# Two of five gate-and-up chunks as seven block products of sums, and one pool for the weight tiles

## The chip, the core and the metric

The kernel runs on one core of a Trainium2 chip. The metric is the time of one execution on the device in microseconds (us). The core has a matrix engine (TensorE, PE in the profile), three engines for elementwise work (VectorE, DVE; ScalarE, ACT; GpSimd, POOL) and queues that start transfers (SyncE, SP). They run beside each other, each in its own fixed order of instructions, and wait for each other by semaphores.

## The reference

256 tokens of 1024 features go through two blocks in float32. Block 1 is a feed-forward (f1), a mixer of neighbourhood attention and pools, a second feed-forward (f2) and a per-layer embedding (ple), each with a norm by the sum of squares before and after. Block 2 is twice: a feed-forward, a mixer (gated linear attention, gla, the first time; retention, ret, the second), a feed-forward, each followed by a layer norm of the weighted residual. Its four feed-forwards are called s0 to s3.

```python
def swiglu_2(x, w_in, w_out):
    gate, up = jnp.split(x @ w_in, 2, axis=-1)
    return (jax.nn.silu(gate) * up) @ w_out

    ...
    for i in range(DEPTH_2):
        h = layer_norm(DN_ALPHA * h + 0.5 * swiglu_2(h, ffn_w_in[i, 0], ffn_w_out[i, 0]), ln_g[i, 0], ln_b[i, 0])
        ...
        h = layer_norm(DN_ALPHA * h + m, ln_g[i, 1], ln_b[i, 1])
        h = layer_norm(DN_ALPHA * h + 0.5 * swiglu_2(h, ffn_w_in[i, 1], ffn_w_out[i, 1]), ln_g[i, 2], ln_b[i, 2])
```

The inner width of a feed-forward is 2816.

## The kernel before

**Operands.** Every float32 operand of a product is split in two tiles of type float32r that add up to it: `hi` is a copy (ScalarE), `lo` is the operand less `hi` (VectorE). A product of two operands is then three matmuls: hi by hi, hi by lo, lo by hi (`mm3`, L173). The tokens are two blocks of 128, t=0 and t=1.

**Weights.** They are streamed in units of 128x2048 elements, 1 MB. `fetch` (L143) starts the transfer of a unit to a tile `raw`, copies it to `whi` on ScalarE (L155) and subtracts on VectorE to `wlo` (L156). The pools hold 4 raw, 5 whi and 5 wlo tiles. `unit` (L159) hands out the next unit of a fixed plan and fetches one unit ahead.

**A feed-forward.** `ffn` (L336) computes gate and up in five chunks of 512 columns and a sixth of half the size. A chunk of 512 columns has four weight units (gate's two halves of the 1024 rows, up's two), and each serves both blocks of tokens: eight block products [128x512] by [512x512], each of 12 matmuls of 128x512. When a gate is complete, ScalarE makes `sg` (silu, L344 or L347); when the up product is complete, VectorE makes `pr` = up times `sg` (L345 or L348). Four ticks later (a tick is six matmuls) `pr` is transposed on TensorE and split in `hTh` (ScalarE, L192) and `hTl` (VectorE, L193). Then `lagged` (L296) multiplies by the down weight, 11 units of two rows of blocks: t=1 follows t=0 by three units (`LAG`), so that t=0's norm, which `after` starts, can run beside t=1's last products. The norms are `rms_post` (L247) and `rms_in` (L232) in block 1 and `ln_post` (L258) in block 2; `turn_in` (L243) defers the transposes of the normed tokens by `TURN` ticks, and these become `xTh` and `xTl`, the next layer's operand.

**Order.** The program is written as one stream in which `tick`, `defer` and `settle` place the deferred pieces. A scheduler then fixes for every engine one order of instructions, in which it takes account of when tiles of a pool come free. So a pool's size has a say in the order, and the order is what the engines keep to while they run. The file also has `proj` (L285), which multiplies one block of tokens by units, and `Chunks`, by which the mixers do the same as `ffn`.

Of the kernel before, what the change touches and what calls it, by code (L numbers as in the profile page):

```python
# [38 lines left out]
class Split:  # L39
    """A float32 operand as two float32r tiles that add up to it exactly."""  # L40
# [8 lines left out]
def ffn_units(g, u, d):  # L49
# [10 lines left out]

MIX_ORDER = [1, 0, 2, 3, 4, 5, 6, 7]
# [4 lines left out]
def all_units():  # L66
    """Every weight unit in the order of its use."""
# [4 lines left out]
    p += ffn_units("s0g", "s0u", "s0d")  # L72
    p += chunk_units("gin", GLA_ORDER) + [("gout", i) for i in range(4)]
    p += ffn_units("s1g", "s1u", "s1d") + ffn_units("s2g", "s2u", "s2d")
    p += chunk_units("rin", RET_ORDER) + [("rout", i) for i in range(8)]
    return p + ffn_units("s3g", "s3u", "s3d")


class Build:
# [152 lines left out]
    def rms_in(self, t, gpre):  # L232
        """The next layer's operand from h[t]: h * g, transposed and split, and its rstd."""
# [24 lines left out]
    def ln_post(self, t, acc, g, b, half, last=False):  # L258
        """h[t] = layer_norm(ALPHA * h + (0.5 if half else 1) * acc) * g + b; its transpose, split."""
# [13 lines left out]
        for n in range(2):  # L273
# [5 lines left out]
            else:  # L279
                self.turn_in(xT, t, n, y)  # L280
# [55 lines left out]
    def ffn(self, xT, r, wg, wu, wd, after, first=False):  # L336
# [14 lines left out]
        pss = {}  # L351
# [670 lines left out]
```

## Time and profile before

| | us |
|---|---|
| median of 3 runs | 1642.52 |
| lowest and highest run | 1640.35, 1642.58 |
| span of the profiled execution | 1639.3 |
| TensorE busy in it | 1622.8 |
| VectorE busy | 935.0 |
| ScalarE busy | 723.9 |
| GpSimd busy | 131.1 |

The span reaches from the first instruction to the last in one execution that the hardware profiler recorded; that execution's own time outside the span is not in the profile. A matmul's busy time in the profile overlaps its neighbour's, so the distance of two starts, not the duration, says how fast they follow each other. "Idle before, releaser" names the time an engine stood still ahead of an instruction and what ended it.

### The profile page before, as it was taken

The numbers are of one execution on the slowest core, as the hardware profiler recorded it, in microseconds if no ns is written. First come the engines' busy times: TensorE is split into PE (matmuls) and PEld (weight loads), VectorE is DVE, ScalarE is ACT, GpSimd is POOL, SyncE is SP. The second block draws the span as 40 slices with busy tenths as digits, with TensorE's granted clock in tenths as the row PEclk, the third lists the DMA queues.
The fourth block names the chain that finished last, engine by engine and source line by source line (L and its number), as shares of the span: only waits on it lengthen the run. The fifth ranks groups of instructions, "written<-read, shape, count | busy, mean of one in ns | idle before, by whom it ended". The sixth has DMA issues, their size and how long they took to land.

```text
span 1639.3 us, 18199 instructions
## 1 busy us (share of the span) xinstructions
PE 1622.8 (99%) x7512; PEld 1339.8 (82%) x7512; DVE 935.0 (57%) x809; ACT 723.9 (44%) x712; POOL 131.1 (8%) x149
## 2 busy tenths in 40 slices
PE   8999999999999999999999999999999999999997
PEld 6888878888888888888888888888887888888886
DVE  6644665565453864537747544654538666485444
ACT  6443554454443754333644433443424444344331
POOL 0000200020000300003011000100003300010000
PEclk9999999999999999999999999999999999999999
DMA  9754654545454564546535454555445544364540
GB/s 356 266 184 154 227 210 143 180 176 210 178 193 158 210 229 177 205 146 214 190 138 213 175 203 149 192 223 206 165 169 206 215 154 166 142 240 172 204 150 30
DMA packets 49650, 308.09 MB, mean 188 GB/s; under 512 B 6032, under 2 KB 7056, under 8 KB 14880
## 3 DMA queue, kind: packets, MB, share of 16 engines
q1 hardware_dynamic: 49568, 306.94, 51.6%
q8 instruction: 59, 0.97, 0.2%
q14 instruction: 23, 0.19, 0.0%
HBM read 305.86 MB, written 1.05 MB: 187 GB/s over the span
## 4 chain that ended last, share of the span: by engine, by line
PE 96%; DVE 2%; issue 1%; ACT 0%; DMA 0%; POOL 0%; DVEq 0%; POOLq 0%; SPq 0%
PE mm L175 21%; PE mm L177 21%; PE mm L176 20%; PE acc L177 9%; PE acc L175 9%; PE acc L176 9%; PE hT L184 2%; DVE wlo L156 1%; PE xT L184 1%; PE tp L184 1%; PE sc L464 1%; PE o L487 0%; DVE bn L265 0%; DVE h L264 0%; PE sT L795 0%
## 5 line engine op out<-in xcount | busy, mean ns | idle before, releaser
L156 DVE TENSOR_TENSOR wlo<-raw,whi 128x2048 fp32r<-128x2048 f32 (+1 forms) x287 | 632.4, 2209 | 481.4 <-ACT whi L155 481.3
L155 ACT CAST whi<-raw 128x2048 fp32r<-128x2048 f32 (+1 forms) x287 | 526.9, 1841 | 558.6 <-PE mm L177 283.3
L175 PE MATMUL mm<-whi,xTh 128*128 128x512 f32 x1296 | 516.4, 398 | 0.0
L177 PE MATMUL mm<-whi,xTl 128*128 128x512 f32 x1296 | 506.0, 391 | 0.5 <-DVE xTl L193 0.5
L176 PE MATMUL mm<-wlo,xTh 128*128 128x512 f32 x1296 | 505.0, 390 | 0.0
L177 PEld LDWEIGHTS mm<-whi,xTl 128*128 128x128 f32 x1296 | 243.2, 188 | 53.3 <-DVE xTl L193 1.3
L175 PEld LDWEIGHTS mm<-whi,xTh 128*128 128x128 f32 x1296 | 243.4, 188 | 50.5 <-issue 2.7
L176 PEld LDWEIGHTS mm<-wlo,xTh 128*128 128x128 f32 x1296 | 243.8, 188 | 47.6
L175 PE MATMUL acc<-whi,hTh 128*128 128x512 f32 x528 | 207.4, 393 | 0.0
L177 PE MATMUL acc<-whi,hTl 128*128 128x512 f32 x528 | 205.7, 390 | 0.0
L176 PE MATMUL acc<-wlo,hTh 128*128 128x512 f32 x528 | 205.6, 389 | 0.0
L177 PEld LDWEIGHTS acc<-whi,hTl 128*128 128x128 f32 x528 | 99.1, 188 | 20.7
L176 PEld LDWEIGHTS acc<-wlo,hTh 128*128 128x128 f32 x528 | 99.2, 188 | 20.1
L175 PEld LDWEIGHTS acc<-whi,hTh 128*128 128x128 f32 x528 | 99.1, 188 | 19.8
L193 DVE TENSOR_TENSOR hTl<-hT,hTh 128x512 fp32r<-128x512 f32 (+1 forms) x72 | 46.3, 643 | 58.8 <-ACT hTh L192 58.8
L175 PE MATMUL mm<-whi,xh 128*128 128x512 f32 x176 | 70.5, 401 | 6.6 <-ACT whi L155 6.6
L176 PE MATMUL mm<-wlo,xh 128*128 128x512 f32 x176 | 69.6, 395 | 0.0
L177 PE MATMUL mm<-whi,xl 128*128 128x512 f32 x176 | 69.4, 394 | 0.0
L204 POOL TENSOR_SCALAR erl<-mv 128x1 f32<-128x1 f32 x12 | 5.1, 423 | 771.5 <-DVE mv L267 771.5
L344 ACT ACTIVATE sg<-mm 128x512 f32<-128x512 f32 (+1 forms) x48 | 26.9, 560 | 86.9 <-issue 56.6
L219 POOL TENSOR_TENSOR v<-ss 128x1 f32<-128x1 f32 x16 | 16.2, 1016 | 529.3 <-ACT jk L213 529.3
L192 ACT CAST hTh<-hT 128x512 fp32r<-128x512 f32 (+1 forms) x72 | 39.3, 546 | 26.0 <-PE hT L184 26.0
(216 smaller groups left out, 1267.4 us busy)
## 6 DMA issues: line engine op xcount, KB each, us to landing
raw<-in_rin SPq DMA_DIRECT2D x24, 1024.0 KB, 4.8
raw<-in_bin SPq DMA_DIRECT2D x16, 1024.0 KB, 4.8
raw<-in_f2g SPq DMA_DIRECT2D x12, 1024.0 KB, 4.8
raw<-in_s0g SPq DMA_DIRECT2D x12, 1024.0 KB, 4.9
raw<-in_gin SPq DMA_DIRECT2D x12, 1024.0 KB, 4.8
raw<-in_s1g SPq DMA_DIRECT2D x12, 1024.0 KB, 4.8
raw<-in_s2g SPq DMA_DIRECT2D x12, 1024.0 KB, 4.8
raw<-in_s3g SPq DMA_DIRECT2D x12, 1024.0 KB, 4.8
```

What stands on the lines that cost most here:

```text
L155: nc.scalar.copy(hi[:, s], raw[:, s])
L156: nc.vector.tensor_tensor(out=lo[:, s], in0=raw[:, s], in1=hi[:, s].bitcast(F32), op=ALU.subtract)
L175: mm(ps, x.hi, w.hi, start=start, stop=False)
L176: mm(ps, x.hi, w.lo, start=False, stop=False)
L177: mm(ps, x.lo, w.hi, start=False, stop=stop)
L184: self.nc.tensor.transpose(ps[:, i * P:(i + 1) * P], src[:, i * P:(i + 1) * P], self.ident)
L192: self.nc.scalar.copy(hi, v)
L193: self.nc.vector.tensor_tensor(out=lo, in0=v, in1=hi.bitcast(F32), op=ALU.subtract)
L204: self.nc.gpsimd.tensor_scalar(out=e, in0=v, scalar1=1.0, scalar2=eps, op0=ALU.mult, op1=ALU.add)
L219: self.nc.gpsimd.tensor_tensor(out=v, in0=st[:, 0:1], in1=st[:, 1:2], op=ALU.add)
L344: nc.scalar.activation(sg[:, :n], ps_g[:, :n], AF.Silu)
L464: nc.tensor.matmul(ps[:, j * SEQ:(j + 1) * SEQ], qT[t][64 * a:64 * a + 64, 2 * b + j, :], kT[b][64 * a:64 * a + 64, j, :], start=True, sto ...
```

## The change

In block 2's four feed-forwards, the chunks 2 and 4 (`SEVEN`) are computed otherwise. Gate and up of both blocks of tokens and both halves of the 1024 rows form a 2 by 2 matrix product of blocks, and `seven` computes it as seven products of sums and differences of blocks (in Winograd's form of Strassen's scheme) instead of eight plain ones. The sums of weight units are made on VectorE by `fetch_sum`: four additions of 128x2048 a chunk, in place in the raw tiles, and seven splits in `hi` and `lo`; the units are fetched three ahead. The differences of the tokens' blocks are made once per feed-forward: `turn_in` keeps copies of the transposes (`xr`, `y3`) and `sums_in` makes four split operands `yT`. The seven products, which lie in PSUM one by one, are put together by `seven` on VectorE (`c11`, `p1`, `u4`, `c22`), and `finish7` makes `sg0` and `sg1` of them, which are then transposed as `pr` is elsewhere.

The pools raw (4), whi (5) and wlo (5) become one pool `w` of 14 tiles, for all units of the program; the pool of small tiles `S` grows from 28 to 30.

```diff
-        out += [(g, 2 * c), (g, 2 * c + 1), (u, 2 * c), (u, 2 * c + 1)]
+        four = [(g, 2 * c), (g, 2 * c + 1), (u, 2 * c), (u, 2 * c + 1)]
+        out += [(four, j) for j in range(7)] if c in seven else four
...
+SEVEN = (2, 4)
...
-    BUFS = {"raw": 4, "whi": 5, "wlo": 5, "S": 28, "mm": 5, "tp": 3, "y": 2, "u": 2,
+    BUFS = {"w": 14, "S": 30, "mm": 5, "tp": 3, "y": 2, "u": 2,
...
+    def W(self, name, dt=F32):
+        return self.T("w", [P, UNIT], dt, name=name)
...
-        raw = self.T("raw", [P, UNIT], F32)
-        hi = self.T("whi", [P, UNIT], F32R)
-        lo = self.T("wlo", [P, UNIT], F32R)
+        if isinstance(name, list):
+            return self.ready.append(self.fetch_sum(name, i))
+        raw, hi, lo = self.W("raw"), self.W("whi", F32R), self.W("wlo", F32R)
...
+    def fetch_sum(self, four, j):
+        nc = self.nc
+        if j == 0:
+            self.sums = {}
+        r = self.sums
+        def load(key, at):
+            r[key] = self.W("raw")
+            nc.sync.dma_start(out=r[key], in_=self.ins[four[at][0]][four[at][1]])
+        def add(to, key):
+            nc.vector.tensor_tensor(out=r[to], in0=r[key], in1=r[to], op=ALU.add)
+        if j == 0:
+            load("a", 0), load("b", 2)
+            key = "a"
+        elif j == 1:
+            load("c", 3)
+            add("a", "b")
+            key = "a"
+        elif j == 2:
+            load("d", 1)
+            add("b", "c")
+            key = "b"
+        elif j == 3:
+            key = "d"
+        elif j == 4:
+            add("a", "c")
+            key = "a"
+        elif j == 5:
+            key = "c"
+        else:
+            add("a", "d")
+            key = "a"
+        hi, lo = self.W("whi", F32R), self.W("wlo", F32R)
+        nc.scalar.copy(hi, r[key])
+        nc.vector.tensor_tensor(out=lo, in0=r[key], in1=hi.bitcast(F32), op=ALU.subtract)
+        return Split(hi, lo)
...
+            if (t, n) != (1, 1):
+                raws[t, n] = self.S([P, CW], name="xr")
+                self.nc.scalar.copy(raws[t, n], ps)
+            if (t, n) == (1, 0):
+                raws[3] = self.S([P, CW], name="y3")
+                self.nc.vector.tensor_tensor(out=raws[3], in0=raws[0, 0], in1=ps, op=ALU.subtract)
+            if (t, n) == (1, 1):
+                raws[1] = raws.pop((1, 0))
+                self.nc.vector.tensor_tensor(out=raws[1], in0=raws[1], in1=ps, op=ALU.subtract)
...
+    def sums_in(self, raws):
+        sub = lambda o, a, b: self.nc.vector.tensor_tensor(out=o, in0=a, in1=b, op=ALU.subtract)
+        r2, r4 = raws.pop((0, 0)), raws.pop((0, 1))
+        sub(r2, r2, raws[1])
+        sub(r4, r4, r2)
+        return {i: self.split(r, 4, "yT") for i, r in ((1, raws.pop(1)), (3, raws.pop(3)), (2, r2), (4, r4))}
...
+    def seven(self, x, y, four, done):
...
+            w = self.unit(four, j, 4, 3)
...
+        p1, c11, u4, c22 = t("u", "p1"), t("u", "c11"), t("y", "u4"), t("y", "c22")
+        nc.scalar.copy(p1, times("P1", x[0][0], 0))
+        p5 = times("P5", y[1], 1)
+        p7 = times("P7", y[3], 2)
+        TT(out=c11, in0=times("P2", x[0][1], 3), in1=p1, op=ALU.add)
+        done(0, c11, None)
+        TT(out=p1, in0=times("P6", y[2], 4), in1=p1, op=ALU.subtract)
+        TT(out=u4, in0=p5, in1=p1, op=ALU.add)
+        TT(out=c22, in0=u4, in1=p7, op=ALU.subtract)
+        TT(out=p1, in0=p1, in1=p7, op=ALU.subtract)
+        TT(out=u4, in0=times("P3", y[4], 5), in1=u4, op=ALU.add)
+        done(1, u4, None)
+        TT(out=p1, in0=times("P4", x[1][1], 6), in1=p1, op=ALU.subtract)
+        done(2, p1, c22)
...
+        def finish7(c):
+            sg = [self.T("sg", [P, CW], F32, name=f"sg{t}") for t in range(NT)]
+            def done(i, a, b):
+                if i == 0:
+                    nc.scalar.activation(sg[0], a, AF.Silu)
+                elif i == 1:
+                    nc.vector.tensor_tensor(out=sg[0], in0=a, in1=sg[0], op=ALU.mult)
...
+            if raws is not None and c in SEVEN:
+                if not y:
+                    y.update(self.sums_in(raws))
+                self.seven(xT, y, [(wg, 2 * c), (wg, 2 * c + 1), (wu, 2 * c), (wu, 2 * c + 1)], finish7(c))
+                continue
```

The fixed order of three engines, before and now, at three places.

VectorE at the end of chunk 1 of s0 and in chunk 2, before (`pr_4509` is the last result of chunk 1, the following `wlo` are units of the chunks 2 and 3):

```order
L345 TENSOR_TENSOR pr_4471<-mm_4445,sg_4470 128x512
L156 TENSOR_TENSOR wlo_4585<-raw_4583,whi_4584 128x2048
L345 TENSOR_TENSOR pr_4509<-mm_4474,sg_4508 128x512
L156 TENSOR_TENSOR wlo_4591<-raw_4589,whi_4590 128x2048
L193 TENSOR_TENSOR hTl_4505<-hT_4499,hTh_4504 128x512
L193 TENSOR_TENSOR hTl_4555<-hT_4549,hTh_4554 128x512
L156 TENSOR_TENSOR wlo_4664<-raw_4662,whi_4663 128x2048
L156 TENSOR_TENSOR wlo_4670<-raw_4668,whi_4669 128x2048
```

and now (L202 are the `lo` of sums, L177 the additions of weight units, L445 is `pr`, L239 the second half of a small split; `pr_4520` is the last result of chunk 1):

```order
L202 TENSOR_TENSOR wlo_4453<-raw_4448,whi_4452 128x2048
L177 TENSOR_TENSOR raw_4448<-raw_4450,raw_4448 128x2048
L445 TENSOR_TENSOR pr_4520<-mm_4485,sg_4519 128x512
L239 TENSOR_TENSOR hTl_4516<-hT_4510,hTh_4515 128x512
L177 TENSOR_TENSOR raw_4450<-raw_4548,raw_4450 128x2048
L239 TENSOR_TENSOR yTl_4526<-xr_4283,yTh_4525 128x512
L202 TENSOR_TENSOR wlo_4552<-raw_4448,whi_4551 128x2048
L239 TENSOR_TENSOR yTl_4530<-y3_4285,yTh_4529 128x512
L202 TENSOR_TENSOR wlo_4559<-raw_4450,whi_4558 128x2048
L239 TENSOR_TENSOR yTl_4534<-xr_4141,yTh_4533 128x512
L177 TENSOR_TENSOR raw_4448<-raw_4548,raw_4448 128x2048
L239 TENSOR_TENSOR yTl_4538<-xr_4158,yTh_4537 128x512
```

Behind the last result of chunk 1 now stand additions and splits of sums of chunk 2, with those of the tokens' differences between them.

TensorE at the end of f1's down product, before (`acc00` and `acc01` are t=0's result, `acc10` and `acc11` t=1's, `xT_1371` the first transposes of the next layer's operand):

```order
L176 MATMUL acc01_1023<-wlo_1263,hTh_1008 128x512
L177 MATMUL acc01_1023<-whi_1262,hTl_1009 128x512
L175 MATMUL acc10_1097<-whi_1172,hTh_822 128x512
L176 MATMUL acc10_1097<-wlo_1173,hTh_822 128x512
...
L177 MATMUL acc10_1097<-whi_1232,hTl_973 128x512
L184 MATMUL xT_1371<-ident_201,u_1326 128x128 x4
L175 MATMUL acc10_1097<-whi_1262,hTh_1057 128x512
...
L184 MATMUL xT_1386<-ident_201,u_1328 128x128 x4
L175 MATMUL acc11_1098<-whi_1232,hTh_972 128x512
```

and now:

```order
L222 MATMUL acc01_1023<-wlo_1263,hTh_1008 128x512
L223 MATMUL acc01_1023<-whi_1262,hTl_1009 128x512
L222 MATMUL acc10_1097<-wlo_1263,hTh_1057 128x512
L223 MATMUL acc10_1097<-whi_1262,hTl_1058 128x512
L221 MATMUL acc10_1097<-whi_1262,hTh_1057 128x512
...
L222 MATMUL acc11_1098<-wlo_1263,hTh_1057 128x512
L223 MATMUL acc11_1098<-whi_1262,hTl_1058 128x512
L230 MATMUL xT_1371<-ident_201,u_1326 128x128 x4
L230 MATMUL xT_1386<-ident_201,u_1328 128x128 x4
L221 MATMUL mm_1453<-whi_1292,xTh_1376 128x512
```

Before, t=1's products on the units that t=0 was ahead by (48 matmuls) stood behind t=0's last, with the transposes among them; now ten of t=1's stand there, and the transposes come after all of them. The end of the down product of s0 to s3 and of f2 reads alike.

ScalarE in chunk 2 of f1, before (`whi` the copies of weight units, `sg` the silu of a gate, `hTh` a small split):

```order
L155 CAST whi_481<-raw_480 128x2048
L347 ACTIVATE sg_476<-mm_372,rs_198 128x512
L155 CAST whi_487<-raw_486 128x2048
L155 CAST whi_552<-raw_551 128x2048
L192 CAST hTh_472<-hT_467 128x512
L155 CAST whi_558<-raw_557 128x2048
L347 ACTIVATE sg_588<-mm_492,rs_187 128x512
L192 CAST hTh_522<-hT_517 128x512
```

and now:

```order
L447 ACTIVATE sg_476<-mm_372,rs_198 128x512
L161 CAST whi_408<-raw_407 128x2048
L238 CAST hTh_472<-hT_467 128x512
L161 CAST whi_481<-raw_480 128x2048
L238 CAST hTh_522<-hT_517 128x512
L447 ACTIVATE sg_588<-mm_492,rs_187 128x512
L161 CAST whi_487<-raw_486 128x2048
L161 CAST whi_552<-raw_551 128x2048
L447 ACTIVATE sg_626<-mm_526,rs_198 128x512
L161 CAST whi_558<-raw_557 128x2048
```

Here `sg` and `hTh` stand between the copies more evenly, and `sg_588` has moved ahead of `whi_487` and `whi_552`.

## Rows read from the trace of the kernel before

**Rows 1.** Page, span and engines: busy time, share, instructions.
```profile
span 1639.3 us, 18199 instructions
PE 1622.8 (99%) x7512; PEld 1339.8 (82%) x7512; DVE 935.0 (57%) x809; ACT 723.9 (44%) x712; POOL 131.1 (8%) x149
```
**Rows 2.** Page, shares of the chain that ended last.
```profile
PE 96%; DVE 2%; issue 1%; ACT 0%; DMA 0%; POOL 0%; DVEq 0%; POOLq 0%; SPq 0%
```
**Rows 3.** Windows over two chunks of s0: window, length, engines' busy time, clock, DMA.
```profile
628.87:651.60 22.73, 22.73 (x105) 18.80 (x104) 11.66 (x8) 9.70 (x9) 0.00 (x0) 1.00 0.49 185
651.60:674.32 22.72, 22.72 (x105) 18.80 (x104) 11.66 (x8) 9.70 (x8) 0.00 (x0) 1.00 0.50 185
```
**Rows 4.** Timeline of TensorE in s0: start, duration, instruction.
```profile
629.12 0.39 PE L177 MATMUL mm<-whi,xTl 128*128 128x512 f32 x1
629.35 0.39 PE L175 MATMUL mm<-whi,xTh 128*128 128x512 f32 x1
```
**Rows 5.** Lines by form: count, busy us, mean ns, idle before and releasers.
```profile
L156 DVE TENSOR_TENSOR wlo<-raw,whi 128x2048 fp32r<-128x2048 f32 x271 | 622.2, 2299 | 479.9 <-ACT whi L155 479.8
L193 DVE TENSOR_TENSOR hTl<-hT,hTh 128x512 fp32r<-128x512 f32 x60 | 41.2, 687 | 50.1 <-ACT hTh L192 50.1
L345 DVE TENSOR_TENSOR pr<-mm,sg 128x512 f32<-128x512 f32 x40 | 27.5, 686 | 18.8 <-PE mm L177 18.7
L155 ACT CAST whi<-raw 128x2048 fp32r<-128x2048 f32 x271 | 517.7, 1913 | 554.3 <-PE mm L177 283.3 <-PE acc L177 212.6 <-issue 42.1
L344 ACT ACTIVATE sg<-mm 128x512 f32<-128x512 f32 x40 | 23.8, 595 | 69.3 <-issue 42.5 <-PE mm L177 26.8
L347 ACT ACTIVATE sg<-mm,rs 128x512 f32<-128x512 f32 x20 | 13.7, 686 | 27.7 <-issue 17.8 <-PE mm L177 9.5 <-POOL rs L205 0.5
```
**Rows 6.** Timeline of VectorE in s0, at 594 and at 641 us.
```profile
594.50 4.50 DVE L156 TENSOR_TENSOR wlo<-raw,whi 128x2048 fp32r<-128x2048 f32 x2 [0.81 <-ACT whi L155]
...
641.69 2.29 DVE L156 TENSOR_TENSOR wlo<-raw,whi 128x2048 fp32r<-128x2048 f32 x1 [3.97 <-ACT whi L155]
643.90 0.68 DVE L345 TENSOR_TENSOR pr<-mm,sg 128x512 f32<-128x512 f32 x1
644.51 2.28 DVE L156 TENSOR_TENSOR wlo<-raw,whi 128x2048 fp32r<-128x2048 f32 x1
```
**Rows 7.** Timeline of TensorE at the end of s0's down product.
```profile
748.82 0.39 PE L177 MATMUL acc<-whi,hTl 128*128 128x512 f32 x1
...
760.89 0.39 PE L175 MATMUL mm<-whi,xTh 128*128 128x512 f32 x1
```
**Rows 8.** Timeline of VectorE there.
```profile
750.68 1.28 DVE L264 SCALAR_TENSOR_TENSOR h<-acc,h 128x512 f32<-128x512 f32 x2
...
754.80 1.40 DVE L276 SCALAR_TENSOR_TENSOR y<-h,rl,ln_b 128x512 f32<-128x512 f32 x2
756.12 2.28 DVE L156 TENSOR_TENSOR wlo<-raw,whi 128x2048 fp32r<-128x2048 f32 x1
758.33 1.30 DVE L193 TENSOR_TENSOR xTl<-xT,xTh 128x512 fp32r<-128x512 f32 x2
```
**Rows 9.** Timeline of ScalarE, then of VectorE, at the end of f1.
```profile
183.37 0.60 ACT L213 ACTIVATE jk<-acc 128x512 f32<-128x512 f32 x1
...
185.83 1.41 DVE L255 SCALAR_TENSOR_TENSOR y<-acc,rp,ffn_post_g 128x512 f32<-128x512 f32 x2 [1.00 <-POOL rp L205]
```
**Rows 10.** Timeline of TensorE at the start of the program.
```profile
6.58 0.80 PE L175 MATMUL mm<-whi,xh 128*128 128x512 f32 x1 [6.58 <-ACT whi L155]
...
9.60 0.63 PE L175 MATMUL mm<-whi,xh 128*128 128x512 f32 x1
10.03 0.63 PE L176 MATMUL mm<-wlo,xh 128*128 128x512 f32 x1
```

More of the change, by code (lines that the diff above doesn't have):

```diff
@@ L46, in __getitem__, with ffn_units @@
         return Split(self.hi[i], self.lo[i])
-def ffn_units(g, u, d):
+def ffn_units(g, u, d, seven=()):
     out = []
     for c in range(5):
-        out += [(g, 2 * c), (g, 2 * c + 1), (u, 2 * c), (u, 2 * c + 1)]
+        four = [(g, 2 * c), (g, 2 * c + 1), (u, 2 * c), (u, 2 * c + 1)]
+        out += [(four, j) for j in range(7)] if c in seven else four
     return out + [(g, 10), (g, 11)] + [(d, i) for i in range(11)]
@@ L71, in all_units @@
     p += [("pgate", i) for i in range(4)] + [("pproj", 0)]
-    p += ffn_units("s0g", "s0u", "s0d")
+    p += ffn_units("s0g", "s0u", "s0d", SEVEN)
     p += chunk_units("gin", GLA_ORDER) + [("gout", i) for i in range(4)]
-    p += ffn_units("s1g", "s1u", "s1d") + ffn_units("s2g", "s2u", "s2d")
+    p += ffn_units("s1g", "s1u", "s1d", SEVEN) + ffn_units("s2g", "s2u", "s2d", SEVEN)
     p += chunk_units("rin", RET_ORDER) + [("rout", i) for i in range(8)]
-    return p + ffn_units("s3g", "s3u", "s3d")
+    return p + ffn_units("s3g", "s3u", "s3d", SEVEN)
 class Build:
@@ L241, in rms_in, with turn_in, turn @@
         return xT, self.row_rstd(t)
-    def turn_in(self, xT, t, n, u):
-        self.defer(TURN[t] + n, lambda: xT.__setitem__(n, self.splitT(u)))
+    def turn_in(self, xT, t, n, u, raws=None):
+        def turn():
+            ps = self.transpose4(u, 4, "xT")
+            xT[n] = self.split(ps, 4, "xT")
+            if raws is None:
+                return
+            if (t, n) != (1, 1):
[7 more added lines that the diff above has]
+                self.nc.vector.tensor_tensor(out=raws[1], in0=raws[1], in1=ps, op=ALU.subtract)
+        self.defer(TURN[t] + n, turn)
+    def sums_in(self, raws):
[4 more added lines that the diff above has]
+        return {i: self.split(r, 4, "yT") for i, r in ((1, raws.pop(1)), (3, raws.pop(3)), (2, r2), (4, r4))}
     def rms_post(self, t, acc, gpost, half):
@@ L256, in rms_post, with ln_post @@
             nc.vector.tensor_tensor(out=h[:, sl], in0=h[:, sl], in1=y, op=ALU.add)
-    def ln_post(self, t, acc, g, b, half, last=False):
+    def ln_post(self, t, acc, g, b, half, last=False, raws=None):
         nc, h = self.nc, self.h[t]
@@ L279, in ln_post @@
             else:
-                self.turn_in(xT, t, n, y)
+                self.turn_in(xT, t, n, y, raws)
                 self.nc.gpsimd.tensor_scalar(out=h[:, sl], in0=y, scalar1=ALPHA, scalar2=0.0, op0=ALU.mult, op1=ALU.add)
@@ L294, in proj, with times @@
                 self.tick()
+    def seven(self, x, y, four, done):
+        nc, TT = self.nc, self.nc.vector.tensor_tensor
+        t = lambda tag, name: self.T(tag, [P, CW], F32, name=name)
+        def times(name, x, j):
+            ps = self.M(name)
+            w = self.unit(four, j, 4, 3)
+            for k in range(4):
+                self.mm3(ps, x[:, k, :], w[:, k, :], k == 0, k == 3)
+                if k % 2:
+                    self.tick()
+            return ps
+        p1, c11, u4, c22 = t("u", "p1"), t("u", "c11"), t("y", "u4"), t("y", "c22")
[12 more added lines that the diff above has]
+        done(2, p1, c22)
     def lagged(self, x, name, n_units, after, lag=LAG, have=None, extra=None):
@@ L334, in lagged, with ffn @@
         after(1, acc[1])
-    def ffn(self, xT, r, wg, wu, wd, after, first=False):
+    def ffn(self, xT, r, wg, wu, wd, after, first=False, raws=None):
         nc = self.nc
@@ L349, in finish @@
             self.defer(4, lambda: hT.__setitem__((t, c), self.splitT(pr, n // P, "hT")))
-        pss = {}
+        def finish7(c):
[5 more added lines that the diff above has]
+                    nc.vector.tensor_tensor(out=sg[0], in0=a, in1=sg[0], op=ALU.mult)
+                    self.defer(4, lambda: hT.__setitem__((0, c), self.splitT(sg[0], 4, "hT")))
+                else:
+                    nc.scalar.activation(sg[1], a, AF.Silu)
+                    nc.vector.tensor_tensor(out=sg[1], in0=b, in1=sg[1], op=ALU.mult)
+                    self.defer(4, lambda: hT.__setitem__((1, c), self.splitT(sg[1], 4, "hT")))
+            return done
+        pss, y = {}, {}
         if first:
@@ L886, in after, with ln_layer @@
                 h = self.h[t][:, n * CW:(n + 1) * CW]
-                self.turn_in(nx[t], t, n, h)
+                self.turn_in(nx[t], t, n, h, raws)
             self.defer(TURN[t] + 1, lambda: nc.gpsimd.tensor_scalar(out=self.h[t], in0=self.h[t], scalar1=ALPHA, scalar2=0.0, op0=ALU.mult, op1=ALU.add))
         self.ple(xT, r, self.gain("gq", "ple_post_g"), after)
-        def ln_layer(body, i, half, last):
+        def ln_layer(body, i, half, last, raws):
             g, b = self.gain("gp", f"ln_g{i}"), self.gain("gq", f"ln_b{i}")
@@ L896, in after @@
             def after(t, acc):
-                xT[t] = self.ln_post(t, acc, g, b, half, last)
+                xT[t] = self.ln_post(t, acc, g, b, half, last, raws)
             body(after)
@@ L904, in run @@
                 f = 2 * (i // 3) + (i % 3) // 2
-                body = lambda after: self.ffn(nx, None, f"s{f}g", f"s{f}u", f"s{f}d", after)
+                body = lambda after: self.ffn(nx, None, f"s{f}g", f"s{f}u", f"s{f}d", after, raws=raws)
             elif i == 1:
@@ L909, in run @@
                 body = lambda after: self.ret(nx, after)
-            nx = ln_layer(body, i, i % 3 != 1, i == 5)
+            raws_next = {} if i in (1, 2, 4) else None
+            nx = ln_layer(body, i, i % 3 != 1, i == 5, raws_next)
+            raws = raws_next
 def units(w, kb, n):
```

2 lines of the change are left out of this document (1 added, 1 removed).

## The prediction

> **What bounds the kernel now.** I read the page's engine totals first: TensorE is busy for 1622.8 us of a span of 1639.3 us, VectorE for 935.0 and ScalarE for 723.9 [rows 1]. Then the shares of the chain of waits, of which TensorE holds 96% [rows 2]. Then two windows over two gate-and-up chunks of s0, the first feed-forward of block 2: 22.73 and 22.72 us, TensorE busy throughout, VectorE for 11.66 us of each, the granted clock 1.00, the upper of its two levels, 2.4 GHz [rows 3]. So TensorE sets the pace, and the others keep up with half of their time free.
>
> What one product costs is read from starts, not from durations: a 128x512 product lasts 0.39 us in its record, but the next starts 0.23 us later [rows 4]. A chunk has 96 of them and two groups of four transposes; (22.73 - 2 x 0.45) / 96 gives 0.227 us. A block product is twelve: 2.72 us. The Trainium skill ("Perfetto Trace Analysis", Identifying the Most-Contended Engine) calls matmul busy time a bad metric, since matmuls are pipelined; the two starts agree. Priced by the record, eight block products would be 8 x 12 x 0.39 = 37 us, by starts they are 21.8, and the starts are what I use.
>
> **What is removed.** Each of the eight sevened chunks (two in each of four feed-forwards) loses one block product in eight: 8 x 2.72 = 21.8 us, if TensorE stays the bound there. That is the whole possible gain.
>
> **What VectorE gets in return.** A weight unit costs it one `lo` of 128x2048: 2299 ns alone [rows 5], 2.21 us apiece in a row (two in 4.50 us) [rows 6]. Small 128x512 operations cost 687 and 686 ns alone [rows 5], some 0.61 in a row. An addition of two weight units has no row; it is the same operation class on as many float32 elements, two operands read and one written, so I take 2.21 us. Bounds: 1.91, a copy of that size on ScalarE, and 4 x 0.687 = 2.75, four small ones one by one [rows 5]; over all 28 additions (seven per feed-forward are in the walk below) that is -8 to +15 us. A sevened chunk needs 7 `lo` and 4 additions, eleven heavy operations where a plain one needs 4.
>
> They cannot all be done early. VectorE works in its written order, and there `pr_4520`, which waits for chunk 1's last product, stands ahead of all additions of chunk 2 but one. Of before's row one sees the same habit: `pr` between two `lo` [rows 6]. So I walk VectorE from the end of chunk 1 to the first `lo` of chunk 3, without which chunk 3 doesn't get past its first product. Chunk 2: 3 additions and 7 `lo` = 10 x 2.21 = 22.1; 15 small ones (hTl, four yTl, seven combinations and gates, further splits) x 0.61 = 9.2; some 0.6 of waiting for products: 31.9 us, against 22.7 before [rows 3]: +9.2. Chunk 4: 4 additions and 8 `lo` = 26.5; 12 small = 7.3; it can start 2.5 us before chunk 3 ends, and waits about 1 us: 32.3, +9.6. TensorE alone would need 7 x 2.72 + 0.7 = 19.7. Per feed-forward +18.8, four times: **+75 us**. The subtractions in `turn_in` and `sums_in` and ScalarE's copies are small and beside other work, apart from the four yTl that are counted.
>
> **What the shared pool does to the order.** Raw, hi and lo of a unit now draw on one pool of 14, and the static order comes out otherwise, in block 1 too, which has no sevened chunk. Two places.
>
> Layer boundaries. Before, after the last product of the first block of tokens (t=0) of s0's down product, starting at 748.82, TensorE has 12 us of t=1's products left, until 760.89, when the next layer's first product starts without a gap [rows 7]. In those 12 us VectorE does the norm of t=0 and splits its transposes [rows 8], and nothing of it shows. Now t=0 and t=1 alternate, and only ten products of t=1, 2.3 us, stand behind t=0's last; the transposes come after them. What was hidden is exposed. Layer norm: from h to y's end is 750.68 to 756.12 = 5.44; two `lo` of 2.2 stand in VectorE's order before the splits, where before there was one [rows 8], 4.4; transposes, `xTh` and the first `xTl` (as hTl, 0.69 [rows 5]) 1.7: 11.5 less 2.3 = 9.2 us, at s0 to gla, s1 to s2, s2 to ret, ret to s3: 36.8. Sum-of-squares norm: from the second `jk` at 183.37 to y at 185.83 is 2.5 [rows 9]; y, h, one `lo`, h, u 5.2; transposes and splits 1.8: 9.5 less 2.3 = 7.2, three times in block 1: 21.6. gla to s1 has a shorter down product: 4.5 by my count of what stands behind it. At the end of the program t=0's norm, 5.44 us of VectorE, now starts 2.3 us ahead of t=1's and delays it: 3.2. Sum **+66 us**. Bounds: nothing, if the norms slip in elsewhere; and up to 12 each if t=1's chain is late as well, 8 x 12 = 96.
>
> Plain chunks. In ScalarE's order a gate's activation, which waits for a product's end, now stands ahead of `whi` of the next unit, where before several `whi` came first. From that product's end to the first use of `lo` there are some 14 products, 3.2 us; needed are `sg` 0.6 to 0.7, `whi` 1.91, `lo` 2.30 and 0.1 of signalling [rows 5]: 5.0. So about 1.8 us is lost per gate where it holds: two or three times in f1 and in f2, once in each block 2 chunk 3, at the first unit of the down products 0.7, some units in mixer, gla and ret. I count 35 us: **+35**, bounds 0 (where ScalarE is ahead anyhow) and 60.
>
> **The clock.** At the start, after 6.58 us of idling, TensorE's products start 0.43 us apart for ten products [rows 10], then at the 0.23 of [rows 4]; that costs 2 us. Idle times of 7 to 9 us at eight boundaries may each bring that back: 0 to 16, I take 7, as not every idle time is as long as that of the start.
>
> **Sum.** 1639.3 + 75 + 66 + 35 + 7 = 1822 us of span; the median of the runs, 1642.5, stands 3.2 over the profiled span: **1825 us**.
>
> **Rivals.**
> 1. Only VectorE in the sevened chunks counts, and the boundaries and plain chunks stay covered. For it: ScalarE and VectorE have half their time free [rows 1]. Against it: their order is fixed, and a free engine behind a waiting instruction doesn't work. 1639.3 + 75 + 3 = 1717.
> 2. The clock drops beyond the restarts: TensorE, idle for a third of each sevened chunk in pieces of some us, runs its products 0.43 us apart there. At 0.43 apart all through, a sevened chunk's 84 products take 36.1 and its transposes 0.7, 4.7 more than the 32.1 that VectorE sets: 8 x 4.7 = 38, and with the 9 that the clock's term leaves out at the boundaries 1825 + 47 = 1872. For it: the start of the program [rows 10]; against it: no row of before shows a stretch with short gaps. The Trainium skill ("TensorE: Matmul & The Clock Gate", HAM oscillation) describes kernels in which idle time between groups of products re-throttles TensorE and halves its rate; by that this rival would hold, and only the start's rows bear on it here.
> 3. The other side, faster: VectorE gets far enough ahead that TensorE stays the bound. It decides where VectorE can start a sevened chunk's additions 12 us before the chunk ahead ends (31.9 less 19.7); it has 11 us free in that chunk [rows 3]. Then 21.8 us go, and if the boundaries are covered too, 1642.5 - 21.8 = 1621. Against it: `pr` in its order.
>
> **How the numbers follow.** Forecast 1825 with 0.66; rival 1 0.13; rival 2 0.15; faster 0.04; anything between, 0.02. The forecast's own bounds: the boundary and plain terms at a third of their value, -67, give 1758; all at their upper ends, +30 +25 +9, give 1889; that the addition is at its dear end too I leave out. The 80% range takes 1735 to 1890: rival 1's time lies under it, rival 2's in it. A difference of 0.2% (3.3 us) can be told from no change by such a measurement; faster than that 0.04, within 0.01, slower 0.95, since every case but rival 3 adds more than 70 us.
>
> **What would show it.** Windows over chunk 2 and 4 of s0: 31 to 33 us each, VectorE busy in over nine tenths, TensorE's idle time ended by VectorE's `wlo`; rival 3 would show 19.7 us and a full TensorE. An addition of about 2.2 us in the list of lines. At each layer boundary an idle time of TensorE of 7 to 10 us before the first transposes and `mm`, ended by the norm's last step; rival 1 shows none. In f1's and f2's chunks, idle times of 1 to 2 us before products that read `wlo`. Products with starts 0.43 apart only in some after boundaries; rival 2 shows them inside the sevened chunks. The prediction is wrong if block 1, up to s0, takes as long as before, or if the sevened chunks take under 25 us.

## The result and the profile after

The changed kernel takes 1908.74 us (median of 4 runs, 1905.54 to 1913.07) where the kernel before takes 1642.55: a ratio of 1.1623, 95% interval 1.1605 to 1.1642. It is slower by 266 us; 182 were forecast, with a range that ended at 1890. The direction and the places of the loss were right, its size was not.

The page's totals, and below them the shares of the chain that ended last:

```profile
span 1903.7 us, 18172 instructions
PE 1705.9 (90%) x7416; PEld 1364.2 (72%) x7416; DVE 1110.5 (58%) x953; ACT 778.6 (41%) x772; POOL 112.4 (6%) x149
...
PE 44%; DVE 16%; ACT 2%; issue 1%; DMA 1%; POOL 1%; DVEq 0%; POOLq 0%; SPq 0%; ACTq 0%
```

Against [rows 1, 2] TensorE holds 44% of the chain instead of 96%. Its idle time went from 16.5 us (1639.3 - 1622.8) to 197.8. And its busy time grew by 83 us although it has 96 products less, which would take 21.8 us: 105 us of busy time are new. Some 16 of them are the ends of records that no next record overlaps (101 idle times in TensorE's timeline, 0.39 - 0.23 = 0.16 us each); the other 89 us are products and transposes that follow each other more slowly. 181.3 + 104.9 - 21.8 = 264.4, the difference of the two spans. The forecast was almost all idle time; nearly a third of the 286 us that were lost is TensorE going slower.

The same by layer, from windows between the first products of the layers (before, changed kernel, and the kernel with the shared pool alone, which is the first experiment):

| | before | changed | shared pool alone |
|---|---|---|---|
| f1 | 188.35 | 206.29 | 211.11 |
| mixer of block 1 | 163.37 | 178.12 | 178.25 |
| f2 | 186.74 | 213.44 | 213.68 |
| ple | 29.08 | 48.65 | 49.49 |
| s0 | 186.77 | 222.84 | 200.01 |
| gla | 110.54 | 117.51 | 117.16 |
| s1 | 186.80 | 230.74 | 209.55 |
| s2 | 187.23 | 227.51 | 208.69 |
| ret | 198.98 | 220.22 | 217.80 |
| s3 | 194.86 | 231.80 | 213.18 |

Block 1, which has no sevened chunk, lost 79 us. Three windows over the chunks 2, 3 and 4 of s0 answer to [rows 3] (columns as there; the last decimal numbers are the granted clock, the DMA's share and GB/s):

```profile
701.28:730.94 29.66, 23.44 (x95) 17.41 (x93) 28.84 (x24) 16.98 (x15) 0.00 (x0) 0.94 0.38 142
730.94:758.12 27.18, 23.58 (x108) 18.57 (x106) 13.89 (x10) 9.98 (x9) 0.00 (x0) 1.00 0.43 155
758.12:791.83 33.71, 25.52 (x96) 18.98 (x93) 29.04 (x22) 15.20 (x11) 0.00 (x0) 0.85 0.33 124
```

In the sevened chunks (first and third row) VectorE is busy for 28.84 of 29.66 us and 29.04 of 33.71 (97% and 86%; over nine tenths were forecast), and TensorE waits. The plain chunk between takes 27.18 in place of 22.7, although VectorE has half of it free. VectorE's timeline around chunk 2:

```profile
701.19 0.69 DVE L445 TENSOR_TENSOR pr<-mm,sg 128x512 f32<-128x512 f32 x1
...
702.78 2.28 DVE L177 TENSOR_TENSOR raw<-raw 128x2048 f32<-128x2048 f32 x1
704.98 0.69 DVE L239 TENSOR_TENSOR yTl<-xr,yTh 128x512 fp32r<-128x512 f32 x1
705.59 2.28 DVE L202 TENSOR_TENSOR wlo<-raw,whi 128x2048 fp32r<-128x2048 f32 x1
...
730.70 0.69 DVE L393 TENSOR_TENSOR p<-P,p 128x512 f32<-128x512 f32 x1 [0.28 <-PE P L223]
731.30 2.28 DVE L162 TENSOR_TENSOR wlo<-raw,whi 128x2048 fp32r<-128x2048 f32 x1
```

From chunk 1's last `pr` to chunk 3's first `lo` VectorE works nearly without a gap: 701.19 to 733.58, 32.4 us, where the walk gave 31.9. An addition costs as much as a `lo` (lines by form: count, busy us, mean ns):

```profile
L162 DVE TENSOR_TENSOR wlo<-raw,whi 128x2048 fp32r<-128x2048 f32 x239 | 546.8, 2298 | 291.9 <-ACT whi L161 291.6
L202 DVE TENSOR_TENSOR wlo<-raw,whi 128x2048 fp32r<-128x2048 f32 x56 | 126.6, 2284 | 4.5 <-ACT whi L201 4.5
L177 DVE TENSOR_TENSOR raw<-raw 128x2048 f32<-128x2048 f32 x32 | 73.1, 2285 | 0.2
```

TensorE at the end of f1, which answers to [rows 7] by its kind (t=1's last product, the transposes, the next layer's first products):

```profile
205.15 0.39 PE L223 MATMUL acc<-whi,hTl 128*128 128x512 f32 x1
210.74 1.97 PE L230 MATMUL xT<-ident,u 128*128 128x128 f32 x8 [5.21 <-DVE u L285]
212.87 0.79 PE L221 MATMUL mm<-whi,xTh 128*128 128x512 f32 x1 [0.16 <-ACT xTh L238]
...
214.96 0.79 PE L223 MATMUL mm<-whi,xTl 128*128 128x512 f32 x1 [0.87 <-DVE xTl L239]
215.56 0.63 PE L221 MATMUL mm<-whi,xTh 128*128 128x512 f32 x1
215.98 0.63 PE L222 MATMUL mm<-wlo,xTh 128*128 128x512 f32 x1
```

The exposed norm ends the idle time; from the last product's start to the next layer's first it is 7.7 us, where it was 0.23. The last two rows start 0.42 us apart, the half rate of [rows 10].

A plain chunk of f1, on ScalarE, VectorE and TensorE:

```profile
64.69 0.69 ACT L447 ACTIVATE sg<-mm,rs 128x512 f32<-128x512 f32 x1 [4.94 <-PE mm L223]
65.28 3.70 ACT L161 CAST whi<-raw 128x2048 fp32r<-128x2048 f32 x2
...
67.21 4.50 DVE L162 TENSOR_TENSOR wlo<-raw,whi 128x2048 fp32r<-128x2048 f32 x2 [6.16 <-ACT whi L161]
...
67.23 0.73 PE L221 MATMUL mm<-whi,xh 128*128 128x512 f32 x2
69.56 0.50 PE L222 MATMUL mm<-wlo,xh 128*128 128x512 f32 x1 [1.59 <-DVE wlo L162]
```

ScalarE stood for 4.94 us with a weight unit on chip, because `sg`, ahead in its order, waited for a product; then came the copy, then the split, and TensorE stood for 1.59 us. From `sg`'s start to the product that reads `wlo` it is 4.87 us; the forecast had 5.0.

### The profile page after: what moved, and what is told of

Same layout as the page of the kernel before. It is cut to its first block, busy times and chain, and to the rows that moved or that the text cites. A ratio compares the mean times of both kernels' runs of the same rounds, so it can differ in the third digit from the quotient of the medians.

```text
span 1903.7 us, 18172 instructions
## 1 busy us (share of the span) xinstructions
PE 1705.9 (90%) x7416; PEld 1364.2 (72%) x7416; DVE 1110.5 (58%) x953; ACT 778.6 (41%) x772; POOL 112.4 (6%) x149
## 4 chain that ended last, share of the span: by engine, by line
PE 44%; DVE 16%; ACT 2%; issue 1%; DMA 1%; POOL 1%; DVEq 0%; POOLq 0%; SPq 0%; ACTq 0%
PE mm L222 8%; PE mm L223 8%; PE mm L221 8%; PE acc L222 5%; PE acc L223 5%; PE acc L221 5%; DVE wlo L202 5%; DVE wlo L162 3%; DVE raw L177 3%; ACT whi L161 1%; PE P L222 1%; PE P L221 1%; PE P L223 1%; ACT whi L201 1%; DVE h L333 1%
## 5 line engine op out<-in xcount | busy, mean ns | idle before, releaser
L162 DVE TENSOR_TENSOR wlo<-raw,whi 128x2048 fp32r<-128x2048 f32 (+1 forms) x255 | 557.2, 2197 | 292.8 <-ACT whi L161 292.3
L161 ACT CAST whi<-raw 128x2048 fp32r<-128x2048 f32 (+1 forms) x255 | 462.0, 1826 | 178.8 <-DMA raw<-in_f2d 18.8
L222 PE MATMUL mm<-wlo,xTh 128*128 128x512 f32 x1040 | 419.3, 404 | 33.1 <-DVE wlo L162 33.1
L221 PE MATMUL mm<-whi,xTh 128*128 128x512 f32 x1040 | 417.3, 409 | 6.4 <-ACT whi L161 5.8
L223 PE MATMUL mm<-whi,xTl 128*128 128x512 f32 x1040 | 414.7, 400 | 9.0 <-DVE xTl L239 8.9
L221 PEld LDWEIGHTS mm<-whi,xTh 128*128 128x128 f32 x1040 | 200.2, 194 | 56.7 <-ACT whi L161 11.7
L201 ACT CAST whi<-raw 128x2048 fp32r<-128x2048 f32 x56 | 105.5, 1905 | 67.3 <-DVE raw L177 67.3
L202 DVE TENSOR_TENSOR wlo<-raw,whi 128x2048 fp32r<-128x2048 f32 x56 | 126.6, 2284 | 4.5 <-ACT whi L201 4.5
L221 PE MATMUL P<-whi,yTh 128*128 128x512 f32 x128 | 59.6, 466 | 44.2 <-ACT whi L201 44.2
L177 DVE TENSOR_TENSOR raw<-raw 128x2048 f32<-128x2048 f32 x32 | 73.1, 2285 | 0.2
L445 DVE TENSOR_TENSOR pr<-mm,sg 128x512 f32<-128x512 f32 (+1 forms) x32 | 19.9, 621 | 87.3 <-PE mm L223 68.9
```

The lines of the kernel that those rows point to most:

```text
L161: nc.scalar.copy(hi[:, s], raw[:, s])
L162: nc.vector.tensor_tensor(out=lo[:, s], in0=raw[:, s], in1=hi[:, s].bitcast(F32), op=ALU.subtract)
L177: nc.vector.tensor_tensor(out=r[to], in0=r[key], in1=r[to], op=ALU.add)
L201: nc.scalar.copy(hi, r[key])
L202: nc.vector.tensor_tensor(out=lo, in0=r[key], in1=hi.bitcast(F32), op=ALU.subtract)
L221: mm(ps, x.hi, w.hi, start=start, stop=False)
```

## The experiments

Each was run beside the kernel before on the same chip; ratios are to it, with the 95% interval.

**The shared pool alone.**

```diff
-    BUFS = {"raw": 4, "whi": 5, "wlo": 5, "S": 28, "mm": 5, "tp": 3, "y": 2, "u": 2,
+    BUFS = {"w": 14, "S": 28, "mm": 5, "tp": 3, "y": 2, "u": 2,
...
-        raw = self.T("raw", [P, UNIT], F32)
-        hi = self.T("whi", [P, UNIT], F32R)
-        lo = self.T("wlo", [P, UNIT], F32R)
+        raw = self.T("w", [P, UNIT], F32, name="raw")
+        hi = self.T("w", [P, UNIT], F32R, name="whi")
+        lo = self.T("w", [P, UNIT], F32R, name="wlo")
```

> The kernel before, with its three weight pools (4, 5 and 5 tiles) made one pool of 14, and no sevened chunk. Theory P (the shared pool's order is the greater part of the loss): block 1 loses the 79 us that it lost in the changed kernel, gla 7, ret 21, and each of the four feed-forwards of block 2 some 18 to 27, as f1 and f2 did: 1642 + 107 + 90 = about 1838 us. Rival V (the sums on VectorE are the greater part, as in the forecast): the pool costs no more than the forecast's 66 + 35 + 7 = 108: about 1750 us.

Measured: 1826.84 us, 1.1111 (1.1094 to 1.1127), 183 us over the 1644.08 of before beside it. The pool is the greater part of the loss; the sevened chunks add some 82. Theory P's number was 11 us high, and rival V falls.

**Seven products with the three pools of before.**

```diff
-    BUFS = {"w": 14, "S": 30, "mm": 5, "tp": 3, "y": 2, "u": 2,
+    BUFS = {"raw": 4, "whi": 5, "wlo": 5, "S": 30, "mm": 5, "tp": 3, "y": 2, "u": 2,
...
-        return self.T("w", [P, UNIT], dt, name=name)
+        return self.T(name, [P, UNIT], dt, name=name)
```

> The changed kernel with the three pools of before (raw 4, whi 5, wlo 5) in place of the shared one; its sevened chunks are kept whole. Theory P: t=1 follows t=0 by three units again (48 products behind t=0's last), and in VectorE's order seven of the heavy operations of a sevened chunk stand ahead of the last result of the chunk before, where the changed kernel has two; TensorE stays the bound and the 21.8 us are mostly won: 1621 to 1650 us. Rival V (eleven heavy operations a chunk bind VectorE whatever the order): +75, 1717 us.

Measured: 1641.71 us, 0.9988 (0.9979 to 0.9998). With the lag back, and seven heavy operations ahead of `pr`, 75 us of VectorE's binding are gone: rival V falls. But the 21.8 us are not there. TensorE in chunk 2 of s0, between the products P1 and P5:

```profile
625.83 0.50 PE L221 MATMUL P<-whi,yTh 128*128 128x512 f32 x1 [2.56 <-ACT yTh L238]
...
627.48 0.50 PE L223 MATMUL P<-whi,yTl 128*128 128x512 f32 x1 [0.63 <-DVE yTl L239]
...
628.89 0.63 PE L221 MATMUL P<-whi,yTh 128*128 128x512 f32 x1
629.32 0.63 PE L222 MATMUL P<-wlo,yTh 128*128 128x512 f32 x1
```

It waits for the splits of the tokens' differences, and then goes at half rate for a while: about 5.5 us, in each of the four feed-forwards.

**The differences earlier.** To that kernel:

```diff
-            if raws is not None and c in SEVEN:
-                if not y:
-                    y.update(self.sums_in(raws))
+            if raws is not None and not y:
+                y.update(self.sums_in(raws))
+            if raws is not None and c in SEVEN:
```

> The sevened kernel with three pools, with the tokens' differences (the four yT splits and two subtractions) issued at the start of chunk 1 instead of chunk 2. Theory: in the run with three pools the only stall of TensorE in a feed-forward of block 2 stood in chunk 2 between P1 and P5, 2.56 + 0.63 us of idling and some 2 us of half rate after it, about 5.5 us in all, which is what a feed-forward had won by its two sevened chunks (5.4); without it the 21.8 us come through: about 1620 us. Rival: VectorE is busy for 97% of these chunks, and what leaves one place of its order is late at another: 1635 to 1642 us.

Measured: 1620.87 us, 0.9865 (0.985 to 0.9879): the whole possible gain. A window over chunk 2 of s0:

```profile
619.80:640.00 20.20, 20.20 (x94) 16.77 (x93) 20.20 (x14) 15.31 (x11) 0.00 (x0) 1.00 0.59 218
```

TensorE and VectorE are both busy for all of it. VectorE has 14 operations in this window, where the changed kernel has 24 in its 29.66 us: the others come earlier.

**Without the additions**, under the shared pool:

```diff
-            nc.vector.tensor_tensor(out=r[to], in0=r[key], in1=r[to], op=ALU.add)
+            return
```

> The changed kernel with its shared pool, without the 32 additions of weight units on VectorE (the seven products are taken of single units, so this part of the computation is left out). If VectorE's work bounds the sevened chunks under this order, 7 additions per feed-forward leave the path: 28 x 2.2 = 62 us less, 1847 us. If the chunks are bound by what the order makes wait, for which the additions are only one of several things ahead of a copy, a third of that: about 1885 us.

Measured: 1833.02 us, 1.1137 (1.1112 to 1.1161), 76 us less than the changed kernel, in which the additions are busy for 73.1 us. Under that order the additions are on the path in full, as the first theory had it (with 62 us), and without them the kernel takes 6 us more than with the shared pool alone. The other work that the seven products add on VectorE stayed in; no run prices it by itself.

**Filled boundaries.**

```diff
+    def busy(self, n, acc):
+        self.nc.scalar.copy(self.wm, acc[0][:, :256])
+        ps = self.TP("wm")
+        for i in range(n):
+            self.nc.tensor.matmul(ps[:, :256], self.wm[:, :P], self.wm, start=True, stop=True)
...
+                if t == 0 and not last:
+                    self.busy(40, acc)
```

> The changed kernel with 40 matmuls of 128x256 (4.5 us) on TensorE behind t=0's last product at eight layer boundaries; their results aren't used. If the half rate after these idle times is on the path, the some ten products and the transposes that start 0.43 us apart come at the full rate: 2 to 3 us each, 16 to 24 in all: about 1887 us. If t=1's products, which now end 4.5 us later, were what the next layer waits for, it comes out slower: up to 1940 us. If neither: 1909 us.

Measured: 1911.32 us, 1.1625 (1.1607 to 1.1644). About the time of the changed kernel (1908.74). TensorE at the end of f1:

```profile
205.69 5.00 PE L237 MATMUL wm<-wm 128*128 128x256 f32 x40
...
214.65 1.23 PE L230 MATMUL xT<-ident,u 128*128 128x128 f32 x8 [1.66 <-DVE u L291]
217.05 0.77 PE L221 MATMUL mm<-whi,xTh 128*128 128x512 f32 x1 [1.18 <-ACT xTh L244]
...
219.48 0.63 PE L221 MATMUL mm<-whi,xTh 128*128 128x512 f32 x1
219.90 0.63 PE L222 MATMUL mm<-wlo,xTh 128*128 128x512 f32 x1
```

The idle time fell from 5.21 to 1.66 us, and the next products started 0.42 us apart all the same: here, and at the other ends of layers in block 1, the half rate was not, or not all, taken away, and the run doesn't tell what it costs there. At three boundaries of block 2 (s1 to s2, s2 to ret, ret to s3) it was. Ten us from the first transposes behind s1 on, in the changed kernel and in this one:

```profile
1222.38:1232.38 10.00, 8.22 (x24) 6.16 (x25) 9.93 (x12) 3.95 (x5) 5.01 (x5) 0.54 0.22 73
...
1221.04:1231.04 10.00, 8.48 (x43) 6.34 (x42) 10.00 (x14) 4.57 (x7) 5.80 (x5) 1.00 0.12 44
```

The granted clock is 1.00 in place of 0.54. The first, the 12th and the 96th product of s2, in the changed kernel:

```profile
1224.17 0.80 PE L221 MATMUL mm<-whi,xTh 128*128 128x512 f32 x1
...
1231.17 0.63 PE L223 MATMUL mm<-whi,xTl 128*128 128x512 f32 x1
...
1251.92 0.39 PE L223 MATMUL mm<-whi,xTl 128*128 128x512 f32 x1
```

and here:

```profile
1222.35 0.50 PE L221 MATMUL mm<-whi,xTh 128*128 128x512 f32 x1
...
1226.80 0.40 PE L223 MATMUL mm<-whi,xTl 128*128 128x512 f32 x1
...
1250.17 0.39 PE L223 MATMUL mm<-whi,xTl 128*128 128x512 f32 x1
```

From the first product to the 12th it is 4.5 us in place of 7.0, and to the 96th 27.8 in both; at the other two boundaries the 12th comes after 4.4 us in place of 7.1 and 7.0, and the 96th after 32.45 and 29.00 in place of 32.40 and 27.50. What the clock gave back was lost again in later waits, in s2 in one of 1.57 us for a `whi` at 1239.41 that the changed kernel doesn't have. As far as this run shows, the half rate behind these three boundaries is not on the path, as the third case has it.

**Fifteen tiles in place of fourteen**, to the kernel with the shared pool alone:

```diff
-    BUFS = {"w": 14, "S": 28, "mm": 5, "tp": 3, "y": 2, "u": 2,
+    BUFS = {"w": 15, "S": 26, "mm": 5, "tp": 3, "y": 2, "u": 2,
```

> The run with the shared pool and no sevened chunk again, with 15 tiles in place of 14 (three tiles a unit, so that a raw tile follows a raw tile; the pool of small tiles has 26 for room). The order of every engine is the same, row by row; only what a load and a copy wait for differs: loads wait for VectorE alone, no more for products. Theory L (the loads' waits make the loss): most of the 184 us is gone: 1645 to 1680 us. Rival O (the order makes it, as in the forecast's terms for boundaries and plain chunks, 66 + 35): about 1745 us. If neither the load's wait nor the slots matter: 1827 us.

It followed from SyncE's waits. With fourteen tiles (engine and line, what it waited for: us in total, times, longest):

```profile
SPq L154 <- PE mm L176: 436.3, 78, 8.2
SPq L154 <- PE mm L177: 299.6, 53, 14.4
SPq L154 <- PE acc L177: 223.3, 42, 8.0
SPq L154 <- DVE wlo L156: 197.5, 78, 12.2
```

Loads (L154) waited for products. With fifteen they wait mostly for VectorE, which reads the raw tiles:

```profile
SPq L154 <- DVE wlo L156: 743.8, 154, 10.5
...
SPq L154 <- PE mm L177: 169.8, 33, 9.5
```

Measured: 1826.85 us, 1.1111 (1.1093 to 1.113), the time of fourteen tiles. Theory L falls, and rival O has the cause right: the orders of all five engines are the same in both kernels, and so is the time. What O gave, 1745, is the forecast's size again, and falls with it; 1827 is the number of the third case.

**Which tiles share.** Raw apart, and whi and wlo in one pool of ten, with the sevened chunks:

```diff
-    BUFS = {"w": 14, "S": 30, "mm": 5, "tp": 3, "y": 2, "u": 2,
+    BUFS = {"raw": 4, "w": 10, "S": 30, "mm": 5, "tp": 3, "y": 2, "u": 2,
...
-        return self.T("w", [P, UNIT], dt, name=name)
+        return self.T("raw" if name == "raw" else "w", [P, UNIT], dt, name=name)
```

> The changed kernel with a pool of 4 for raw and a shared pool of 10 for whi and wlo. Theory L (raw tiles in one rotation with hi and lo make the loads wait for products): the loads wait for VectorE's splits again, as before, and the time is that of three pools, about 1642 us. Rival (any sharing upsets the order): over 1750 us.

Measured: 1642.63 us, 1.0002 (0.9992 to 1.0011). That is theory L's number, but its reason falls with the fifteen tiles; that sharing as such costs nothing here is what the run adds. Then, without sevened chunks, raw with wlo, and raw with whi:

```diff
-    BUFS = {"raw": 4, "whi": 5, "wlo": 5, "S": 28, "mm": 5, "tp": 3, "y": 2, "u": 2,
+    BUFS = {"w": 9, "whi": 5, "S": 28, "mm": 5, "tp": 3, "y": 2, "u": 2,
...
```

> The kernel before with raw and wlo in one pool of 9 and whi in its own of 5; no sevened chunk. TensorE's order is, row by row, that of the pool of 14. Theory O (the order alone makes the loss): 1827 us, as with 14 and with 15 tiles. Rival (the number of tiles that a load must wait for has a part): more than 10 us away from it.

```diff
-    BUFS = {"raw": 4, "whi": 5, "wlo": 5, "S": 28, "mm": 5, "tp": 3, "y": 2, "u": 2,
+    BUFS = {"w": 9, "wlo": 5, "S": 28, "mm": 5, "tp": 3, "y": 2, "u": 2,
...
```

> The kernel before with raw and whi in one pool of 9 and wlo in its own of 5; no sevened chunk. In TensorE's order t=1 follows t=0 by three units again (48 products behind t=0's last). Theory O (it is the pairing of raw and wlo, by which the next unit's load is placed behind this unit's split on VectorE, that upsets the order): 1642 to 1660 us. Rival (any sharing by raw tiles costs most of it): over 1750 us.

Measured: raw with wlo 1822.72 us, 1.1095 (1.1078 to 1.1111); raw with whi 1644.07, 1.001 (1.0001 to 1.002). With raw and wlo in one pool all five engines run through the same sequence of operations as with the pool of fourteen. With raw and whi in one pool the loads wait for products as well:

```profile
SPq L154 <- PE mm L177: 825.9, 163, 11.0
```

and it costs nothing, so the loads' waits are not what costs the time. Nor is it sharing as such or the number of tiles: a pool that holds both raw and wlo gives the order that costs 180 us. That order on three separate pools was not run; the fifteen tiles, where loads mostly wait for the reader of a raw tile, come nearest to it. Why the scheduler orders so is not shown; that a unit's load is there placed behind the split of the unit before is a reading of the code.

**Further chunks.** From the kernel with three pools and early differences: f2's chunks 2 and 4 too, and, apart from that, chunk 3 of block 2's feed-forwards too:

```diff
-    p += ffn_units("f2g", "f2u", "f2d")
+    p += ffn_units("f2g", "f2u", "f2d", SEVEN)
...
+            def sc(t):
+                return {} if r is None else {"scale": r[t]}
...
```

> The kernel with three pools and early differences, and chunks 2 and 4 of f2 in block 1 sevened as well (its rows are scaled by the norm after the products, so the sums can be made of the unscaled tokens). If TensorE stays the bound, two more block products go: 2 x 2.72 = 5.4 us under 1620.9, 1615.5 us. If something in f2 (the scaled gate and product on VectorE) makes it wait: 1621 us or more.

```diff
-SEVEN = (2, 4)
+SEVEN = (2, 3, 4)
```

> The kernel with three pools and early differences, with chunks 2, 3 and 4 of block 2's feed-forwards sevened in place of 2 and 4. Theory (VectorE's reserve between two sevened chunks is what carries them): chunk 3 adds 3 lo, 4 additions and some 6 small operations, 19 us, where VectorE had about 3 us free from chunk 2 to chunk 4; with what chunks 1 and 5 take up, 8 to 16 us more in each of four feed-forwards: 1652 to 1685 us. Rival (TensorE stays the bound): four more block products go, 1620.9 - 10.9 = 1610 us.

Measured: with f2 1615.66 us, 0.9833 (0.9819 to 0.9848), 5 us less than without, as expected, and the best of all runs; with chunk 3 1699.8, 1.0342 (1.0324 to 1.0359). Three windows in a row in s0 in the latter; the first holds chunk 2, and the products of chunk 3 start at 640.29, those of chunk 4 at 670.20:

```profile
619.80:640.50 20.70, 20.70 (x96) 17.11 (x95) 20.70 (x14) 11.76 (x9) 0.00 (x0) 1.00 0.41 153
640.50:662.00 21.50, 17.13 (x67) 12.53 (x66) 20.74 (x17) 10.13 (x9) 0.00 (x0) 0.87 0.17 53
662.00:690.00 28.00, 22.44 (x83) 16.89 (x81) 25.07 (x20) 13.26 (x10) 0.00 (x0) 0.86 0.39 147
```

Chunk 2 goes at TensorE's pace; in the second and third window VectorE is busy for 96% and 90%, and TensorE waits, at a granted clock of 0.87 and 0.86. The loss was 15 us larger than the upper end expected.

## Why the prediction was wrong

**The sevened chunks, +75.** Right. From chunk 1's end to chunk 3's first `lo` it is 32.4 us and over chunk 4 33.7 (31.9 and 32.3 were forecast), and an addition is a `lo`. The changed kernel and the pool alone differ by 82 us, and without the additions it is 76 us less. Rival 1 falls with the 79 us of block 1. Rival 3 fell for this kernel, for the reason given: `pr` stands ahead in VectorE's order. With three pools, and so another order, and the differences early it came true: 1621 was its time, 1620.87 was measured.

**The boundaries, +66.** Right in place and cause, a little high: from the last product of a layer to the next layer's first it is 7.5 us more than before three times, 7.0 to 7.1 four times and 2.0 after gla, 52.8, with idle times of 5.2 us where 7 to 10 were forecast in one piece; at the end 11.4 us lie behind the last product instead of 8.2. Together 56.

**The plain chunks, +35, and the clock, +7.** This is the step that failed. 264.4 of span less 82 and 56 leaves 126, where 42 were forecast. The kernel with the shared pool alone shows it without sevened chunks: each layer's loss in the table, less its boundary, is 15 us in f1, 7 in the mixer, 19 in f2, 20 in ple, 6 in s0, 5 in gla, 16 in s1, 14 in s2, 12 in ret and 15 in s3, some 130 together. The mechanism is the one told (`sg` ahead of `whi`, 5.0 us where 3.2 were there), but the forecast counted too few stalls and priced each at 1.8 us. In f1 four of the five chunks have one: its row shows 1.6 us of idle time, and with the products next to it, whose starts lie further apart too (two take from 67.23 to 69.56 us), a chunk takes 25.0 us in place of 22.7, so 2.3 are lost. Nor did the forecast price the first chunk of a layer. In f2's, t=1's norm follows t=0's on VectorE, TensorE stands another 3.90 us for a `whi` at 405.82 us, and the first `hT` comes 27.7 us behind the first product, before 17.3. And ple, for which the forecast had nothing, lost 19.6 us. TensorE there:

```profile
619.29 1.22 PE L221 MATMUL acc<-whi,xTh 128*128 128x512 f32 x2 [4.01 <-ACT whi L161]
...
621.62 0.80 PE L222 MATMUL acc<-wlo,xTh 128*128 128x512 f32 x1 [1.10 <-DVE wlo L162]
...
632.88 0.74 PE L221 MATMUL mm<-whi,pTh 128*128 128x512 f32 x2 [3.21 <-ACT whi L161]
```

Three idle times for copies and splits of weights, 8.3 us, and slow products behind them.

**The slow products.** In the changed kernel 256 products start 0.38 to 0.48 us ahead of the next one, most of them 0.43, together 51 us over their full-rate spacing (before, 14 products and 2.8 us), where 7 us were forecast for the boundaries. Some 64 of them, 13 us, stand behind boundaries. Rival 2 put them in the sevened chunks, and there are 114, 23 us (granted clock 0.94 and 0.85 in the two windows of s0): its sign came, but not its price of 38 us: the sevened chunks cost 82 us in all, and 75 were forecast from VectorE alone. The rest stand behind short idle times in plain chunks and in ple, where the forecast had none. How much of the 51 us is on the path stays open, but for three boundaries where a run without the half rate gained nothing.

By the account of the Trainium skill ("TensorE: Matmul & The Clock Gate", HAM oscillation) idle time between groups of products halves TensorE's rate; the trace agrees, with products 0.42 us apart behind the 5.21 us of idling at the end of f1.

What the forecast left out was the order's effect on TensorE as a chain: it priced each wait alone, and took the count of places from a few of them.

## What to carry to other kernels

Before a pool is shared between what is loaded and what is made of it, compare the fixed orders of a part that the change does not touch: here block 1, which has no sevened chunk, shows the pool's cost by itself: 79 us. An engine with half its time free can still bind where its order puts new work behind a wait; ask which instruction ahead of it waits, and move the work, as the run with early differences did. Price a stall from start to start, over the products on both sides of it: 1.6 us of idle time in a row were 2.3 us of a chunk here. And follow time that is won up to the next wait: behind three boundaries 2.5 us were won by the 12th product and gone by the 96th.

## What the runs showed of the hardware

TensorE's half rate can come back after a short idle time, not only after 5 us and more as at layer boundaries and at the start: in a plain chunk of f1, seven products from 95.25 us on start 0.43 us apart, at a granted clock of 0.50 (the lower level, 1.2 GHz), after 1.59 us of idling that ended at 94.59; behind the other three idle times of that length in f1 none did. With 5 us of matmuls that nothing waits for put ahead of it, it came all the same at the end of f1, where idle times of 1.66 and 1.18 us were left, and not at three boundaries of block 2, where 1.5 us were left behind the first products. In the kernel with early differences VectorE is busy for 20.20 of 20.20 us beside a TensorE that is busy for all of it, with no wait of either in that window.
